# Seven block products in place of eight for the first branch's projection, one half of it moved ahead of the second half's input projection, and the last heads' rows of the second branch in the buffers for rows of x

## The chip, the cores and the metric

The kernel is one program on one core of a Trainium2 chip. The metric is the device time of one execution in microseconds (us), the median over runs. The trace of one profiled execution goes with it; its span runs from the first to the last thing that the profiler recorded.

## What is computed

One layer over 2048 latent tokens of width 1024, with a prefix of 256 context tokens. A combined input projection feeds a gated convolution (branch A) and a bidirectional mLSTM with 8 heads (branch B). Each branch is projected, the two are merged by sigmoid gates, and an output projection, a gated residual and a norm close the layer.

```
hx = rmsnorm(x, g_norm) * (1 + scale) + shift
px = hx @ w_in + b_in
h_x = mlstm_bidir(px[..., :STATE_COLS], ctx_states)      # 8 heads, two directions
...
y_a = b_a * conv * silu(z_a)
y_b = sigmoid(o) * hn * silu(z_b)
merged = sigmoid(g_a) * (y_a @ w_pa) + sigmoid(g_b) * (y_b @ w_pb)
out = x + gate * (merged @ w_out + b_out);  return rmsnorm(out, g_final)
```

All inputs are float32. A dense product is made in three matmul passes on operands split into a rounded high part and a low rest (high by high, high weight by low data, low weight by high data). The split of each operand costs one copy on ScalarE (ACT) and one subtraction on VectorE (DVE): `split`, L178 and L179.

## The kernel before, in words

**Halves and blocks.** The tokens are worked in two halves of 1024 (half 0, half 1), data being held with channels on the partitions. Most dense products are made by `pair` (the matmul is L427): two output tiles of 128 channels for both 512-token column blocks, in seven block products of 12 matmuls instead of eight (Strassen and Winograd's scheme). Its moving operand is an `Operands` object: seven blocks in 28 buffers x0 to x27, loaded by 14 DMAs of 512 KB and 14 splits. The three sums of blocks that this needs are made beforehand by `combine` (L295), which reads a scratch tensor, subtracts on DVE and writes the sums beside it; the sums of weights are made on GpSimd (POOL, L360) in `Stream`. The other form is `slab` (L474): one output tile, for the two column blocks one after the other, 48 matmuls straight from `Branch` (whole rows of y for k = 0 to 7, hi and lo).

**Stages in time.** (1) Input projection of half 0, 44 pairs. Beside it the second half's operands are prepared (`prep_b`, scratch xod), w_out is scaled by the gate (`late_rows`, scratch wod), and the states of the context and of one direction are scanned (`ctx_scan`, `state_scan`, with the state update matmul L658). (2) Input projection of half 1, 44 pairs, beside it `state_scan` and `scan` of half 1 and, for the first EARLY = 3 heads, `scan` of half 0. (3) Four branch products made of slabs: w_pa on half 1 (`PaEnd`), w_pb on half 1 (`PbEnd`), w_pa on half 0, w_pb on half 0, each 8 slabs of 48 matmuls. Beside the first three runs the late `scan` of the remaining five heads of half 0. (4) The output projection in 8 pairs with the residual and the last norm (`output`, `begin`, `close`).

**The order of the work.** On TensorE (PE) the order is the program's order. `run(dense, rate, urate)` writes one dense matmul after the other and puts in between, `rate` steps per matmul, steps of the queue `later` (scans, preparation) and `urate` steps of `urgent` (loads and splits that are needed soon). `flush` empties a queue. On the other engines a scheduler at build time sets the order, save for instructions wrapped in `pin`, which keep the program's. All loads and stores of note go through one DMA queue, that of SyncE (SP), in order.

**Names used below.** `scan` with late=True makes one chunk of 128 tokens of one head in about nine steps: a product of k and q (L834), the weighted values into pn (L891, L892), the normalisation on DVE and ACT (L897 to L905, hb is the result), and after four chunks four transposes (L849), a product with the gate (L851) and a store to ybd (L852). `Branch.fetch` (L1482) loads rows of ybd and splits them. gb and gf (L1554, L1555) are the two rows that the end of the kernel adds and multiplies with; xt are the rows of x that `begin` (L1576) loads for the output, and wod the blocks of w_out. In `output`, L1604 and L1605 add the products to xt, L1607 squares and sums, and `close` (L1596, stores L1597) applies the norm.

## Time and profile before

| what | value |
|---|---|
| median of 3 runs | 2660.72 us (2659.01 to 2660.84) |
| the profiled execution, its time and its span | 2660.47 us, span 2658.7 us |
| PE, DVE, ACT, POOL busy | 2594.5, 1722.6, 1099.0, 1123.8 us |
| matmuls recorded | 12807 |
| mean granted TensorE clock | 0.994 |
| mean DMA rate | 170 GB/s |

The span is 1.8 us shorter than the execution's own time, and that time lies 0.25 us below the median. PE is the engine to read: it is without work for 64 us of the span, at the start, in short waits in stages 1 and 2, at the start of the output stage and behind the last matmul. A row of the timeline has its start, its length, engine, line and tiles; in square brackets stands the engine's idle time before it and what ended that. A matmul's own length overlaps the next one's; what a stage costs is the distance between starts.

### The profile page before, as it was taken

Reading aid. Unit: us, or ns where it says so; the run is one execution under the profiler, and the core shown is the slowest. Engines: PE = TensorE matmul, PEld = TensorE weight load, DVE = VectorE, ACT = ScalarE, POOL = GpSimd, SP = SyncE. Lnnn points to the kernel's source line nnn. Section 1 sums busy time; section 2 is a strip of 40 time slices with the busy share of each in tenths; the row PEclk is TensorE's granted clock in tenths of the full one; section 3 lists DMA queues with packets and bytes.
Section 4 is the critical chain, followed back from the end, with each engine's and each line's share of the span. In section 5 each row is a group of like instructions: output and inputs, shape, how many; then the busy total and the mean of one; then the engine's idle time right before and its main releaser. Section 6 shows DMA issues by size and latency. Waiting matters only on the chain.

```text
span 2658.7 us, 38177 instructions
## 1 busy us (share of the span) xinstructions
PE 2594.5 (98%) x12807; PEld 2166.7 (81%) x12807; DVE 1722.6 (65%) x3119; ACT 1099.0 (41%) x2269; POOL 1123.8 (42%) x1322
## 2 busy tenths in 40 slices
PE   8999999999999999999999999999999999999998
PEld 7788887888878787877887888888888888888777
DVE  6643237687776777478578577667666656554597
ACT  5433344333333335344443444344444544442233
POOL 1221223233345553235555555565555124422674
PEclk9999999999999999999999999999999999999999
DMA  8333344655734457435644653653566978768542
GB/s 231 101 101 106 106 139 131 211 167 179 232 118 123 139 145 236 118 100 159 195 142 130 201 160 120 195 174 128 154 195 201 301 219 273 253 194 288 195 159 96
DMA packets 373217, 452.99 MB, mean 170 GB/s; under 512 B 24428, under 2 KB 273948, under 8 KB 373020
## 3 DMA queue, kind: packets, MB, share of 16 engines
q1 hardware_dynamic: 372784, 450.46, 54.4%
q8 instruction: 102, 1.67, 0.3%
q14 instruction: 95, 0.78, 0.1%
q10 hardware_dynamic: 236, 0.08, 0.0%
HBM read 319.42 MB, written 131.03 MB: 169 GB/s over the span
## 4 chain that ended last, share of the span: by engine, by line
PE 48%; DVE 3%; DMA 2%; issue 1%; POOL 1%; ACT 0%; SPq 0%; DVEq 0%; POOLq 0%; ACTq 0%
PE pd L427 29%; PE pd L474 11%; PE pn L891 2%; PE pn L892 2%; PE pa L834 1%; PE pu L658 1%; DMA mgd<-t2k 1%; DVE wl L179 1%; PE pa L849 1%; PE pn L658 0%; PE pa L669 0%; DVE xt L1596 0%; DVE xt L1605 0%; DMA x<-wod 0%; DVE cv L999 0%
## 5 line engine op out<-in xcount | busy, mean ns | idle before, releaser
L427 PE MATMUL pd<-x,wh 128*128 128x512 f32 x5320 | 1695.9, 397 | 15.9 <-DVE xt L1605 8.5
L427 PEld LDWEIGHTS pd<-x,wh 128*128 128x128 f32 x5320 | 985.1, 189 | 209.9 <-issue 19.4
L427 PE MATMUL pd<-x,wl 128*128 128x512 f32 x2660 | 1057.3, 397 | 0.0
L427 PEld LDWEIGHTS pd<-x,wl 128*128 128x128 f32 x2660 | 501.8, 189 | 99.3 <-issue 0.2
L178 ACT CAST wh<-sw 128x512 fp32r<-128x512 f32 x382 | 237.0, 620 | 492.9 <-PE pd L427 409.0
L179 DVE TENSOR_TENSOR wl<-sw,wh 128x512 fp32r<-128x512 f32 x382 | 303.2, 795 | 182.0 <-ACT wh L178 177.1
L178 ACT CAST wh<-wr 128x512 fp32r<-128x512 f32 x350 | 216.6, 619 | 375.3 <-PE pd L427 269.9
L360 POOL TENSOR_TENSOR sw<-wr,sw 128x512 f32<-128x512 f32 x95 | 136.1, 1433 | 432.6 <-DVE wl L179 345.2
L179 DVE TENSOR_TENSOR wl<-wr,wh 128x512 fp32r<-128x512 f32 x350 | 289.7, 828 | 42.5 <-ACT wh L178 39.1
L474 PE MATMUL pd<-x,wh 128*128 128x512 f32 x896 | 281.7, 396 | 0.0
L360 POOL TENSOR_TENSOR sw<-wr 128x512 f32<-128x512 f32 x95 | 130.9, 1378 | 236.9 <-DVE wl L179 236.0
L653 POOL TENSOR_SCALAR vw<-tk,wk 128x129 f32<-128x129 f32 x205 | 161.9, 794 | 120.2 <-PE pn L658 109.7
L474 PEld LDWEIGHTS pd<-x,wh 128*128 128x128 f32 x896 | 166.3, 188 | 32.1
L474 PE MATMUL pd<-x,wl 128*128 128x512 f32 x448 | 173.4, 397 | 0.0
L186 POOL TENSOR_SCALAR ssq<-ssq 128x1 f32<-128x1 f32 x128 | 37.2, 291 | 293.7 <-ACT hf L906 289.8
L926 DVE TENSOR_TENSOR t2k<-pd,u 128x512 f32<-128x512 f32 x168 | 115.5, 688 | 59.8 <-PE pd L427 59.1
L360 POOL TENSOR_TENSOR sw<-sw,wr 128x512 f32<-128x512 f32 x94 | 132.4, 1408 | 47.9 <-DVE wl L179 37.4
L904 ACT ACTIVATE hf<-pn,rd 128x128 f32<-128x128 f32 x128 | 47.0, 367 | 246.9 <-DVE rd L900 222.4
L360 POOL TENSOR_TENSOR sw<-wr,wr 128x512 f32<-128x512 f32 x94 | 132.2, 1406 | 20.2 <-DVE wl L179 10.8
L820 POOL TENSOR_SCALAR_AFFINE_SELECT mw<-mw 128x256 f32<-128x256 f32 x128 | 61.7, 503 | 119.5 <-DMA mw<-mwd 89.1
L891 PE MATMUL pn<-tk,pt 128*128 128x129 f32 x512 | 98.8, 275 | 5.0 <-DVE hb L905 5.0
L891 PEld LDWEIGHTS pn<-tk,pt 128*128 128x128 f32 x512 | 86.8, 190 | 16.2 <-issue 5.8
(259 smaller groups left out, 3317.5 us busy)
## 6 DMA issues: line engine op xcount, KB each, us to landing
wr<-in_w_in_dram SPq DMA_DIRECT2D x176, 512.0 KB, 4.1
tk<-tokd SPq DMA_DIRECT2D x64, 386.0 KB, 3.6
mw<-mwd SPq DMA_DIRECT2D x44, 512.0 KB, 5.3
qkd<-t2k SPq DMA_DIRECT2D x64, 256.0 KB, 2.9
qk<-qkd SPq DMA_DIRECT2D x64, 256.0 KB, 3.8
tk<-tokd SPq DMA_DIRECT2D x48, 257.0 KB, 2.9
tokd<-t2k SPq DMA_DIRECT2D x32, 258.0 KB, 2.9
x<-in_w_ada_dram SPq DMA_DIRECT2D x16, 512.0 KB, 6.4
```

What stands on the lines that cost most here:

```text
L178: a = nc.scalar.copy(hi, raw)
L179: b = (eng or nc.vector).tensor_tensor(lo, raw, hi.bitcast(F32), op=OP.subtract)
L186: nc.gpsimd.tensor_scalar(dst, ss, 1.0 / n, EPS, op0=OP.mult, op1=OP.add)
L360: nc.gpsimd.tensor_tensor(s, a, b, op=op)
L427: nc.tensor.matmul(ps[b], op[wi][:, kk, :], xs.at(o, xi, kk), start=(fresh and kk + pi == 0), stop=(o == last[b] and kk == 3 and pi == 2), ...
L474: nc.tensor.matmul(pss[j], ops[k // 4][wi][:, k % 4, :], y(xi, k, j), start=(k + pi == 0), stop=(k == NK - 1 and pi == 2))
L653: pin(nc.gpsimd.tensor_scalar(vw, tk[:, VT], wk, None, op0=OP.mult))
L820: pin(nc.gpsimd.affine_select(mws[m][:, :, 0, d, :], mws[m][:, :, 0, d, :], pattern=[[0, 2], [s, P]], base=0, channel_multiplier=-s, compa ...
L891: nc.tensor.matmul(pn[:, d, :], pt[:, d, :], tk[:, VT], start=True, stop=False)
L892: nc.tensor.matmul(pn[:, d, :], qw[:, d, :], cur if d == carried else tk[:, ST], start=False, stop=True)
L904: nc.scalar.activation(hf, pn[:, 0, 0:P], AF.Copy, scale=rd[:, 0:1])
L926: nc.vector.tensor_tensor(t, ps, add, op=OP.add)
```

## The change

- **w_pa in pairs.** `PaEnd` and the slabs of w_pa go. `Gated` makes w_pa by `pair`, four pairs of seven block products for each half, from `Operands` loaded from yad. For this yad is laid out in blocks (`fin_ba` writes it so), and `combine` runs on it for each half, for half 0 with tiles of the pool of stage 1, for half 1 with the five small buffers cv. Each tile of the gate sad is loaded three tiles ahead into cv, and the result goes to mad, now one tensor for each half.
- **Half 0's w_pa moved** into stage 1, behind the input projection of half 0 and ahead of that of half 1. The rate of `later` in stage 1 falls from 0.235 to 0.212. Half 1's w_pa comes behind stage 2, at rate 0.22, and the loads for the next product are spread over its last pair (`arriving`).
- **One more head early.** EARLY is 4, the rate in stage 2 rises from 0.34 to 0.358, and the late scan has four heads. It runs beside w_pa of half 1 (rate 0.22) and w_pb of half 1 (rate 0.55 in place of 0.305).
- **The last branch's rows.** For w_pb on half 0, `Branch` keeps k = 0 to 3 in the x buffers, 4 and 5 in small ones, and 6 and 7 in four of the six xt buffers, whose pool opens when the late scan's pool is closed. Their loads come behind those of gb and gf.
- **The output.** Block 6 of w_out is loaded and split during w_pb of half 0, so four splits are left for the first output pair, not six. Only the first pair's rows of x are loaded ahead; the others follow in the output stage. L1605 is pinned, and in the last pair one `close` is placed after it.

Counted on PE, with like matmuls in a row written together, the program has 11296 rows before and 11200 now.

First place: SP's queue where the last head of the late scan is handed over to w_pb of half 0. The store to ybd is head 7's last; cv, or xk, is where its rows are loaded to. Before:

```order
L852 DMA ybd_135<-g_5885_23848 128x512
L252 DMA x_6023_24497<-wod 128x1024
L1503 DMA mad<-t2k_24315 128x512
L1482 DMA cv_24348<-ybd_135 128x512
L1482 DMA cv_24350<-ybd_135 128x512
L1554 DMA gb<-rowd 128x1024
L1555 DMA gf<-in_g_final_dram 128x1024
```

Now:

```order
L865 DMA ybd_135<-g_6087_24293 128x512
L1558 DMA t2k_24699<-mad_150 128x512
L252 DMA x_6207_24825<-wod 128x1024
L1611 DMA gb<-rowd 128x1024
L1612 DMA gf<-in_g_final_dram 128x1024
L1541 DMA xk_24667<-ybd_135 128x1024
L1541 DMA xk_24670<-ybd_135 128x1024
```

The loads of gb and gf stood behind those of head 7's rows and now stand ahead of them, and head 6's rows have moved down to the same place.

Second place: DVE in the first output pair, from the split of the second block on (x are the blocks of w_out, u the sums inside a pair, wl the low parts of weights). Before:

```order
L179 TENSOR_TENSOR x_6122_25050<-x_6122_25050,x_6120_25048 128x1024
L179 TENSOR_TENSOR x_6125_25053<-x_6125_25053,x_6123_25051 128x1024
L1605 TENSOR_TENSOR xt_24809<-xt_24809,pd_25071 128x512
L179 TENSOR_TENSOR wl_25136<-sw_25133,wh_25135 128x512
L179 TENSOR_TENSOR x_6126_25054<-x_6126_25054,x_6124_25052 128x1024
L179 TENSOR_TENSOR x_6129_25057<-x_6129_25057,x_6127_25055 128x1024
L441 TENSOR_TENSOR u_25156<-pd_25139,u_25107 128x512
L179 TENSOR_TENSOR wl_25159<-wr_25033,wh_25158 128x512
L179 TENSOR_TENSOR x_6130_25058<-x_6130_25058,x_6128_25056 128x1024
L1604 TENSOR_TENSOR xt_24812<-xt_24812,u_25156 128x512
L179 TENSOR_TENSOR wl_25189<-sw_25186,wh_25188 128x512
L1605 TENSOR_TENSOR xt_24812<-xt_24812,pd_25162 128x512
```

Now:

```order
L179 TENSOR_TENSOR x_6298_25351<-x_6298_25351,x_6296_25349 128x1024
L179 TENSOR_TENSOR x_6301_25354<-x_6301_25354,x_6299_25352 128x1024
L1666 TENSOR_TENSOR xt_25216<-xt_25216,pd_25366 128x512
L179 TENSOR_TENSOR wl_25431<-sw_25428,wh_25430 128x512
L179 TENSOR_TENSOR x_6302_25355<-x_6302_25355,x_6300_25353 128x1024
L454 TENSOR_TENSOR u_25455<-pd_25434,u_25402 128x512
L179 TENSOR_TENSOR wl_25458<-wr_25334,wh_25457 128x512
L1665 TENSOR_TENSOR xt_25219<-xt_25219,u_25455 128x512 x2
L1666 TENSOR_TENSOR xt_25219<-xt_25219,pd_25461 128x512
```

Two of the splits ahead of the second addition to xt are gone from here, and one addition of a sum (the x2) has moved up before it.

The diff, cut to its core:

```diff
     def combine(src, tile=None):
...
-            if kk < 4:
+            if kk < 4 and tile is None:
+                bs[kk] = [vslot() for _ in range(4)]
+                for n, t in enumerate(bs[kk]):
+                    ld.dma_start(t, src[n, :, kk, :])
+            elif kk < 4:
                 bs[kk] = [tile([P, 2, NB]) for _ in range(2)]
...
-    yad = scratch("yad", [NK, P, T])
+    yad = scratch("yad", [8, P, 4, NB])
...
-    mad = dp.tile([NK, P, T], F32, name="mad")
+    mad = scratch("mad", [NK, P, T])
...
-                ld.dma_start(yad[half][n, :, S2[j]], v)
+                ld.dma_start(yad[half][2 * (n // 4) + j, :, n % 4, :], v)
...
+    class Gated:
+        def __init__(self, half):
+            self.half = half
+            self.tiles = [(2 * p + i, j) for p in range(4) for i, j in ((0, 0), (1, 1), (1, 0), (0, 1))]
+            self.s = deque()
+        def load(self):
+            if self.tiles:
+                n, j = self.tiles.pop(0)
+                s = vslot()
+                ld.dma_start(s, sad[self.half][n, :, S2[j]])
+                self.s.append(s)
+        def begin(self):
+            self.st = Stream((w_pa, 2 * p * P, True) for p in range(4))
+            self.st.begin()
+            self.y = Operands()
+            self.y.load(yad[self.half], range(7))
+            for _ in range(3):
+                self.load()
+        def pairs(self):
+            for p in range(4):
+                def fin(i, j, ps, add):
+                    s = self.s.popleft()
+                    nc.vector.scalar_tensor_tensor(s, s, 1.0, added(ps, add), op0=OP.add, op1=OP.mult)
+                    ld.dma_start(mad[self.half][2 * p + i, :, S2[j]], s)
+                    self.load()
+                yield pair(self.st, self.y, fin)
...
     for item, fin, w in todo[kv_end:]:
-        run(pair(st, xA, fin), 0.235, 0.5)
+        run(pair(st, xA, fin), 0.212, 0.5)
+        if w == "B3":
+            urgent.append(combine(yad[0], big))
+    flush(urgent)
+    pa = Gated(0)
+    pa.begin()
+    for dense in pa.pairs():
+        run(dense, 0.212, 0.5)
     flush(urgent)
...
-    EARLY = 3
+    EARLY = 4
...
-        run(pair(st, xB, fin), 0.8 if w in ("q0", "o0", "z0") else 0.34, 0.5)
+        run(pair(st, xB, fin), 0.8 if w in ("q0", "o0", "z0") else 0.358, 0.5)
...
+        if w == "B3":
+            urgent.append(combine(yad[1]))
...
-            if self.region == 0 or k < 6:
-                base = 2 * k if self.region == 0 else 16 + 2 * k
-                hi, lo = [xslot(base + p, [P, T], FR) for p in range(2)]
+            whole = (NK, 6, 4)[self.region]
+            if k < whole or self.region == 2 and k > 5:
+                if k < whole:
+                    base = 2 * k if self.region == 0 else 16 + 2 * k
+                    hi, lo = [xslot(base + p, [P, T], FR) for p in range(2)]
+                else:
+                    hi, lo = [so.tile([P, T], FR, tag="xt", name=nm("xk"), bufs=6) for _ in range(2)]
...
-    class PaEnd:
...
-    RATE, URATE = 0.305, 0.3
...
-    run(branch(w_pa, ya, PaEnd, 1), RATE, URATE)
...
-    run(branch(w_pb, yb, PbEnd, 1), RATE, URATE)
...
-    run(branch(w_pa, ya, PaEnd, 0), RATE, 0.5)
+    pa = Gated(1)
+    pa.begin()
+    ya = Branch(0, lambda k: ybd[1][k], ())
+    def arriving():
...
+    for p, dense in enumerate(pa.pairs()):
+        if p == 3:
+            urgent.append(arriving())
+        run(dense, 0.22, 1.0)
+    flush(urgent)
+    yb = Branch(2, lambda k: ybd[0][k], ())
+    urgent.extend(yb.fetch(k, 24) for k in ready)
+    def heads_done(h):
+        if h < 6:
+            urgent.append(yb.fetch(h))
+    run(branch(w_pb, ya, PbEnd, 1), 0.55, 0.5)
     flush(later)
...
-    urgent.extend(load_wo(o) for o in range(4))
-    urgent.extend(begin(m, 6) for m in range(3))
-    run(branch(w_pb, yb, PbEnd, 0), 0, 0.35)
+    last_heads = [yb.fetch(6, 6), yb.fetch(7, 1)]
+    for f in last_heads:
+        next(f)
+    urgent.extend(last_heads)
+    urgent.extend(load_wo(o) for o in (0, 1, 2, 3, 6))
+    urgent.append(begin(0, 6))
+    run(branch(w_pb, yb, PbEnd, 0), 0, 0.36)
...
-                nc.vector.tensor_tensor(xt[:, s], xt[:, s], ps, op=OP.add)
+                pin(nc.vector.tensor_tensor(xt[:, s], xt[:, s], ps, op=OP.add))
+                if m + 1 == len(tiles):
+                    close()
...
-                if m + 1 == len(tiles):
+                if m + 1 == len(tiles) and (i, j) == (0, 1):
                     close()
...
-                if m == 0 and n in (20, 26, 32, 40, 46, 52):
+                if m == 0 and n in (18, 24, 32, 40):
...
-                if n == 34 and m > 0:
-                    for _ in begin(m + 2):
-                        pass
+                if (m, n) in ((0, 44), (1, 8)) or m > 0 and n == 36:
+                    coming.append(begin(len(xts), 16))
+                step(coming)
```

More of the change, by code (lines that the diff above doesn't have):

```diff
@@ L291, in combine @@
         for kk in range(4):
-            load(kk + 1)
-            (b11, b12), (b21, b22) = [(t[:, 0, :], t[:, 1, :]) for t in bs[kk]]
+            if tile is None:
+                yield from gap(8)
+                b11, b12, b21, b22 = bs[kk]
+            else:
+                load(kk + 1)
+                (b11, b12), (b21, b22) = [(t[:, 0, :], t[:, 1, :]) for t in bs[kk]]
             for d, a, b in ((b11, b12, b11), (b12, b22, b12), (b22, b22, b11), (b21, b21, b22)):
@@ L298, in combine @@
             for n, t in enumerate(bs.pop(kk)):
-                ld.dma_start(src[4 + 2 * n:6 + 2 * n, :, kk, :].rearrange("o p i -> p o i"), t)
+                if tile is None:
+                    ld.dma_start(src[4 + n, :, kk, :], t)
+                else:
+                    ld.dma_start(src[4 + 2 * n:6 + 2 * n, :, kk, :].rearrange("o p i -> p o i"), t)
             yield from gap(4)
+            if tile is None:
+                load(kk + 1)
     class Stream:
@@ L1477, in fetch @@
                 for j in range(2):
-                    hi, lo = [slots[4 * (k - 6) + 2 * j + p](FR) for p in range(2)]
+                    hi, lo = [slots[4 * (k - whole) + 2 * j + p](FR) for p in range(2)]
                     parts.append((hi, lo, self.raw(k)[:, S2[j]]))
@@ L1488, in __call__ @@
             return self.t[p, k, j]
-    class PaEnd:
-        def __init__(self, half, n):
-            self.half, self.n, self.s = half, n, {}
-        def begin(self, j):
-            s = self.s[j] = t2k()
-            ld.dma_start(s, sad[self.half][self.n, :, S2[j]])
-        def end(self, j, ps):
-            s = self.s.pop(j)
-            pin(nc.vector.scalar_tensor_tensor(s, s, 1.0, ps, op0=OP.add, op1=OP.mult))
-            ld.dma_start(mad[self.n, :, S2[j]], s)
     class PbEnd:
@@ L1621, in output @@
         parts = []
-        wo.claim(range(4, 7))
-        for o in range(4, 7):
+        wo.claim((4, 5))
+        for o in (4, 5):
             for q in range(2):
```

24 lines of the change are left out of this document (14 added, 10 removed).

## The prediction

> **What bounds the kernel now.** I read the page's head first, then the chain of waits, then the list of waits.
>
> ```profile
> span 2658.7 us, 38177 instructions
> PE 2594.5 (98%) x12807; PEld 2166.7 (81%) x12807; DVE 1722.6 (65%) x3119; ACT 1099.0 (41%) x2269; POOL 1123.8 (42%) x1322
> ```
>
> PE is at work for 98% of the span, so a change can pay in two ways only: fewer matmuls, or less of the 64.2 us in which PE has none. The other engines have a third of their time free or more. The chain has long stretches of nothing but matmuls, such as this one (start, length, instructions):
>
> ```profile
> 2396.25 40.71 PE pd L474 x180
> ```
>
> From this comes the price of one dense matmul. The last of the 180 lasts 0.40 us and overlaps nothing, so (40.71 − 0.40) / 179 = 0.2252 us from start to start. The list of waits then tells for whom PE waits (sum in us, times, longest):
>
> ```profile
> PE pd L427 <- DVE xt L1605: 8.5, 6, 5.0
> PE pn L658 <- DVE tk L662: 7.4, 6, 3.0
> PE pd L427 <- DVE t2k L926: 5.9, 4, 2.6
> PE pn L891 <- DVE hb L905: 5.0, 2, 2.9
> ```
>
> The largest single wait, 5.0 us for L1605, lies in the output stage, in code that the diff touches. The others are DVE waits of 2 to 3 us beside the scans. None of the four names a DMA.
>
> **The change part by part.** All terms are against the profiled execution, 2660.47 us, which lies 0.25 us below the median of the runs shown. A difference of 0.2%, 5.3 us, is about what a measurement of this kernel can tell from none.
>
> *Matmuls.* The order counts 11296 rows on PE before and 11200 now: 96 fewer. That is what the algebra gives, for each half 8 slabs of 48 (384) against 4 pairs of 84 (336). PE has no slack beside it, so 96 × 0.2252 = **−21.6 us**, the one term with little doubt in it. Should one of those stretches be spoilt by waits, that is a term below.
>
> *The first output pair.* Here are PE's rows and DVE's (start, length, and in brackets the idle time before).
>
> ```profile
> 2498.17 0.50 PE L427 MATMUL pd<-x,wh 128*128 128x512 f32 x1 [1.01 <-DVE x L179]
> 2501.64 0.50 PE L427 MATMUL pd<-x,wh 128*128 128x512 f32 x1 [0.45 <-DVE x L179]
> 2502.67 0.39 PE L427 MATMUL pd<-x,wl 128*128 128x512 f32 x1
> 2508.10 1.19 PE L427 MATMUL pd<-x,wh 128*128 128x512 f32 x2 [5.04 <-DVE xt L1605]
> 2511.45 0.40 PE L427 MATMUL pd<-x,wl 128*128 128x512 f32 x1
> ```
>
> ```profile
> 2500.37 3.45 DVE L179 TENSOR_TENSOR x<-x,x 128x1024 fp32r<-128x1024 f32 x2
> 2504.94 1.21 DVE L179 TENSOR_TENSOR x<-x,x 128x1024 fp32r<-128x1024 f32 x1
> 2507.28 0.67 DVE L1605 TENSOR_TENSOR xt<-xt,pd 128x512 f32<-128x512 f32 x1
> ```
>
> PE stops because its next product needs the bank that L1605 at 2507.28 reads, and L1605 stands on DVE behind splits of w_out. By the order two of those go: the pair row of 3.45 becomes one split of 1.21 (−2.2), the row at 2504.94 goes (−1.2). One weight split leaves and one addition of a sum comes in front, 0.6 us each. That is 3.4 us less in front of L1605; I count 3.3, and a gap of 1.7 us is left. Behind the long gap PE was slow as well:
>
> ```profile
> 2508.00:2512.00 4.00, 3.90 (x11) 3.12 (x12) 2.36 (x4) 1.44 (x4) 1.19 (x3) 0.60 0.00 0
> 457.00:460.00 3.00, 3.00 (x9) 2.35 (x8) 2.49 (x4) 2.12 (x4) 0.00 (x0) 0.54 0.03 8
> 456.10 0.96 PE L427 MATMUL pd<-x,wh 128*128 128x512 f32 x2 [2.65 <-DVE t2k L926]
> 1854.10 0.46 PE L891 MATMUL pn<-tk,pt 128*128 128x129 f32 x2 [2.91 <-DVE hb L905]
> ```
>
> In the first two rows the third number from the end is the granted TensorE clock: 0.60 behind the gap of 5.04 us, 0.54 behind one of 2.65. Eight starts from 2508.10 to 2511.45 took 3.35 us in place of 8 × 0.2252 = 1.80, so a slow restart costs 1.55 us. It doesn't follow every gap: after 2.91 us at 1854.10 the first matmul took 0.46 for two, not 0.96. A gap of 1.7 us is under all that were slow, so I let the restart go too: 3.3 + 1.55 = **−4.85 us**. Bounds: 0 if a load of w_out or the sums take DVE's place in front, −6.6 (5.04 + 1.55) if the whole wait goes. The waits of 1.01 and 0.45 are for two of the four splits that are left, and stay.
>
> *The end.* Behind the last matmul DVE does this:
>
> ```profile
> 2650.39 1.41 DVE L1596 SCALAR_TENSOR_TENSOR xt<-xt,sx,gf 128x512 f32<-128x512 f32 x2 [1.84 <-POOL sx L1614]
> 2651.72 0.68 DVE L1605 TENSOR_TENSOR xt<-xt,pd 128x512 f32<-128x512 f32 x1
> ```
>
> The last addition starts 1.33 us after a norm of another tile that it doesn't need. Pinned ahead of it, it can start when the last product is done, a few tenths after 2650.39: **−1.0 us**, bounds −1.33 and 0.
>
> *The hand-over of head 7.* What costs most among the moved steps:
>
> ```profile
> 2395.65 0.60 PE L849 MATMUL pa<-ident,hb 128*128 128x128 f32 x4
> 2397.00 0.32 SPq L852 DMA_DIRECT2D ybd<-g  x1
> 2401.24 0.80 SPq L1482 DMA_DIRECT2D cv<-ybd  x2
> 2403.52 0.46 SPq L252 DMA_DIRECT2D x<-wod  x1
> 2405.31 1.28 DVE L179 TENSOR_TENSOR cv<-cv,cv 128x512 fp32r<-128x512 f32 x2
> 2407.01 1.07 PE L474 MATMUL pd<-cv,wh 128*128 128x512 f32 x4
> 2412.65 1.05 ACT L178 CAST x<-x 128x1024 fp32r<-128x1024 f32 x1 [3.91 <-DMA x<-wod]
> DMA to landing us min/median/max: 3.4/6.1/8.5
> ```
>
> Head 7's transposes are at 2395.65, its store at 2397.00, and the load of its rows could be issued at 2401.24, 5.6 us after the transposes. The splits ended at 2405.31 + 1.28 = 2406.6, just ahead of 2407.01. Already before there was next to no slack. Now the late scan ends nearer to the product: between the transposes and the first matmul on the low part of head 7's rows the order has 44 dense matmuls, where before it has 50. So the rows are due 0.35 + 44 × 0.2252 = 10.3 us after the transposes. And ahead of them SP now issues gb and gf, then the rows of head 6, each 512 KB, as are head 7's: 2.1 MB where there was 0.5 MB. From 2401.24 to 2412.65 the queue moved cv, gb, gf, a tile of sbd and a block of w_out, 2.36 MB in 11.4 us, so 2.1 MB take 10.1 us. Landing is then at 5.6 + 10.1 = 15.7 us, cast and subtraction of a whole row (1.05 + 1.21) end at 18.0, and PE waits 18.0 − 10.3 = 7.7 us, plus 1.55 for the restart: 9.3. The other end: all four land in the median of such loads (last row), 6.1 us, then the stall is 5.6 + 6.1 + 2.3 − 10.3 = 3.7, and 5.2 with the restart. I take **+7.5 us**, nearer to the row of this very place; bounds 0 (the gates' tiles in front of it delay PE less if rows come early) and +11.
>
> The Trainium skill (DMA: Bandwidth & Descriptors, Queues, rings and completion order) says that on each DMA engine descriptors are consumed in ring order, which speaks against this order of loads, and the trace agrees: the block of w_out issued last of its group landed 9.1 us later. Its Specifications section gives about 358 GB/s as the HBM limit of a core, where this stretch moved 207; by that figure, an estimate, the 2.1 MB take 5.9 us, the stall is 3.5 us, the term +5.0 and the time 2.5 us less.
>
> *Swaps of operands.* Pairs need all seven blocks of a new operand in x. Before, stages of pairs met once ahead of the output; now they meet three times, with w_pa of each half between. At the meeting before:
>
> ```profile
> 1030.48 2.22 DVE L179 TENSOR_TENSOR x<-x,x 128x1024 fp32r<-128x1024 f32 x1
> 1033.10 0.67 PE L658 MATMUL pn<-vw,tk 128*128 128x129 f32 x2 [2.96 <-DVE tk L662]
> ```
>
> A split of 2.22 us on DVE stood before the small L662 for which PE waited 2.96 us. Two more meetings could cost 2 × 2.96 = +5.9, or nothing, since splits of one block (1.21 us) usually fit beside 12 matmuls (2.70 us). I take half of one wait: **+1.5 us**.
>
> *The late scan in front of half 0's last product.* Its rows in the three parts of the stage before (columns: PE, PEld, DVE, ACT, POOL busy, clock, DMA share, GB/s), and the DMAs of the whole of it:
>
> ```profile
> 2076.70:2184.00 107.30, 107.30 (x555) 91.19 (x555) 60.25 (x142) 51.19 (x141) 24.69 (x53) 1.00 0.79 247
> 2184.00:2290.00 106.00, 106.00 (x555) 90.21 (x555) 60.60 (x139) 46.83 (x130) 49.90 (x69) 1.00 0.82 265
> 2290.00:2397.00 107.00, 107.00 (x553) 90.84 (x553) 54.87 (x132) 44.25 (x123) 27.14 (x55) 1.00 0.72 221
> DMA packets 60756, 78.31 MB, mean 244 GB/s; under 512 B 3905, under 2 KB 35649, under 8 KB 60730
> tk<-tokd SPq DMA_DIRECT2D x18, 386.0 KB, 3.9
> qk<-qkd SPq DMA_DIRECT2D x18, 256.0 KB, 4.6
> mw<-mwd SPq DMA_DIRECT2D x18, 256.0 KB, 5.9
> ```
>
> Five heads of eight chunks, 40, took 320.3 us: 8.0 us each. The dense part is 3 × 384 × 0.2252 = 259.4 us, so a chunk's own matmuls cost (320.3 − 259.4) / 40 = 1.52 us. At 0.305 steps a matmul that was 351 steps, 8.8 a chunk. In w_pb of half 1 the rate is now 0.55: 211 steps, 24 chunks, in 384 × 0.2252 + 24 × 1.52 = 123 us, or 5.1 us each. Other work per dense matmul stays. The scan's loads, 18 × 898 KB = 16.6 MB, are 21% of the 78.3 MB; with the stores and gates that go with them I reckon a quarter. Chunks come 8.0 / 5.1 = 1.57 times as fast, so the mean DMA share of 0.78 rises by 0.25 × 0.57, to 0.89. It fits, but with little room, and DVE (0.55 busy) has less too. I take **+3.0 us**, as much as one wait like that at 1854.10; bounds 0 and +12 (0.5 us a chunk).
>
> *Sums of blocks and changed rates.* Before, 32 subtractions made such sums; now 64.
>
> ```profile
> L295 DVE TENSOR_TENSOR xb<-xb,xb 128x512 f32<-128x512 f32 x16 | 14.3, 892 | 0.2
> ```
>
> 32 × 0.85 is 27 us of DVE, beside stages that leave it a third. PE waits where one stands ahead of a scan's step. The rates shift scan steps between stages, so a wait of 2.96 may go or two may come: bounds −3 and +5, I take **+1.0 us**.
>
> Sum: −21.6 − 4.85 − 1.0 + 7.5 + 1.5 + 3.0 + 1.0 = −14.45. 2660.47 − 14.45 = 2646.0, and with the 0.25 us to the median 2646.3 us.
>
> **The rivals.**
> - *Everything added is hidden.* Head 7's rows wait behind nothing, the scan is not disturbed: −21.6 − 4.85 − 1.0 = −27.45, 2633.3 us. For it: DMA landing in 6.1 us, all engines but PE a third idle. Against: no slack at 2407.01 even before. Chance 0.15.
> - *DVE turn-taking eats the gain.* Both meetings cost 2.96 us and sums and scan steps meet: swaps +5.9, rates +5.0, hand-over 9.3, the rest as forecast: −21.6 − 4.85 − 1.0 + 9.3 + 5.9 + 3.0 + 5.0 = −4.25, 2656.5 us, within 0.2%. For it: PE's small waits are all on DVE. Chance 0.13.
> - *The late scan cannot go faster, and it is slower than before.* A chunk is a chain of loads, DVE and ACT steps; if it needs the 8.0 us that it had, w_pb of half 1 is 24 × 2.9 = 70 us longer, and the time is 2646.3 − 3.0 + 70 = 2713 us. It decides from (3.0 + 14.45 + 5.3) / 24 = 0.95 us a chunk more, a chunk of 6.0 us. Against: DMA at 0.89, DVE's free third, and no trace of PE waiting for a scan's DMA. Chance 0.05.
> - That the change doesn't do what it says is closed by the 96 rows.
>
> **How the numbers follow.** The forecast has 0.67. Faster by over 0.2% is below 2655.4 us: the forecast's share (0.64 of 0.67), the first rival and 0.05 of the second: 0.84. Within 0.2%: 0.02 of the forecast, 0.07 of the second, 0.01 of the third: 0.10. Slower: 0.06. The range takes in the first rival's time and the second's: 2633 to 2657 us; outside it lie most of the third, and the ends of the first and second, together some 0.17.
>
> **What would show it.** PE's rows: 12711 or near it. A stretch of dense matmuls starts every 0.225 us. In the first output pair the wait for L1605 is about 1.7 us, and the clock behind it stays at 1. The last addition starts ahead of the norm. Between the last transposes and head 7's first matmuls PE waits 3.5 to 8 us for a split of xk, with the clock at about 0.6 behind it. Chunks in w_pb of half 1 come every 5 us. Wrong would be: PE waiting in w_pb of half 1 for pn or a load by tens of us; no wait at the hand-over; waits of 3 us at each new operand.

## The result, and the profile after

The changed kernel takes 2698.26 us (median of 4 runs, 2695.76 to 2703.19), the kernel before 2660.47: a ratio of 1.0145, 95% interval 1.0128 to 1.0163. It is 38 us slower where 14 us faster was forecast. The profiled execution took 2699.76 us, its span is 2698.0. One of the four executions of e9 below took 11823 us; its ratio leaves that one out.

The head of the page, and PE's largest waits (sum in us, times, longest):

```profile
span 2698.0 us, 38358 instructions
PE 2596.6 (96%) x12711; PEld 2157.6 (80%) x12711; DVE 1815.5 (67%) x3225; ACT 1119.2 (41%) x2288; POOL 1191.1 (44%) x1361
```

```profile
PE pn L904 <- DVE hb L918: 15.5, 11, 2.5
PE pn L671 <- DVE tk L675: 13.7, 11, 3.9
PE pd L487 <- ACT xk L178: 9.3, 1, 9.3
PE pd L440 <- DVE xt L1666: 7.7, 5, 4.2
PE pd L440 <- DVE t2k L939: 5.7, 2, 4.4
```

PE has 96 matmuls fewer, as the order said, and yet its busy time is 2.1 us longer: matmuls behind a long wait run at a lower clock (0.59 granted in the last row of this document, 0.54 and 0.60 in the prediction's) and count as busy. So idle time alone doesn't tell what was lost. Here are both kernels by stage, cut near the first dense matmul of each (to 2 us; columns as in the prediction: length, busy time of PE, PEld, DVE, ACT, POOL, granted clock, DMA share, GB/s). Before: the input projections of half 0 and 1, w_pa and w_pb of half 1, w_pa and w_pb of half 0, the output:

```profile
53.70:1042.00 988.30, 968.23 (x4624) 800.52 (x4623) 626.82 (x971) 390.05 (x668) 338.74 (x325) 0.99 0.47 145
1042.00:2075.60 1033.60, 1019.31 (x5146) 853.67 (x5146) 706.38 (x1472) 453.77 (x1004) 537.00 (x682) 1.00 0.53 163
2075.60:2181.90 106.30, 106.30 (x549) 90.34 (x548) 60.03 (x141) 50.66 (x137) 23.63 (x50) 1.00 0.80 249
2181.90:2290.30 108.40, 108.40 (x567) 92.21 (x566) 62.22 (x141) 48.45 (x134) 50.96 (x71) 1.00 0.82 262
2290.30:2397.00 106.70, 106.70 (x552) 90.62 (x551) 54.57 (x132) 44.25 (x123) 27.14 (x55) 1.00 0.72 221
2397.00:2483.80 86.80, 86.80 (x384) 71.87 (x383) 35.86 (x42) 18.84 (x26) 38.32 (x23) 1.00 0.81 268
2483.80:2658.70 174.90, 156.82 (x676) 126.97 (x675) 147.67 (x164) 64.20 (x131) 97.36 (x89) 0.97 0.40 141
```

After: the input projection of half 0, w_pa of half 0, the input projection of half 1, w_pa and w_pb of half 1, w_pb of half 0, the output:

```profile
52.20:1023.00 970.80, 959.79 (x4583) 794.66 (x4583) 625.05 (x954) 388.15 (x667) 329.81 (x305) 1.00 0.50 152
1023.00:1117.60 94.60, 86.18 (x384) 70.39 (x383) 69.26 (x110) 34.09 (x48) 40.05 (x36) 0.96 0.79 251
1117.60:2187.20 1069.60, 1041.93 (x5246) 868.74 (x5245) 744.13 (x1551) 467.21 (x1050) 563.31 (x724) 0.99 0.58 172
2187.20:2276.50 89.30, 88.10 (x430) 73.23 (x429) 69.71 (x124) 45.12 (x101) 33.81 (x39) 1.00 0.76 242
2276.50:2423.70 147.20, 131.49 (x702) 110.20 (x700) 88.13 (x226) 73.91 (x224) 72.44 (x117) 0.97 0.81 249
2423.70:2524.10 100.40, 91.09 (x386) 73.49 (x384) 38.12 (x43) 19.63 (x26) 32.57 (x21) 0.95 0.74 241
2524.10:2698.00 173.90, 157.32 (x674) 127.54 (x672) 152.07 (x162) 62.31 (x129) 108.56 (x92) 0.97 0.40 138
```

For the losses each stage is cut at its first dense matmul exactly, by count of the dense matmuls. From its length I take what its matmuls ask for: 0.2252 us for a dense one, and 0.122 us for any other, which is what is left for them in the three stages of before in which PE never waits. The rest is the stage's loss, in waits and slow restarts together:

| stage | loss before, us | loss after, us |
|---|---|---|
| start | 14.8 | 13.2 |
| input projection, half 0 | 43.3 | 30.0 |
| w_pa of half 0, between them | | 13.3 |
| input projection, half 1 | 24.8 | 48.9 |
| w_pa of half 1 | −0.2 | 2.4 |
| w_pb of half 1 | −0.4 | 22.2 |
| w_pa of half 0, as slabs | −0.1 | |
| w_pb of half 0 | 0.6 | 14.2 |
| output | 22.8 | 22.3 |

The losses grow from 105.6 to 166.5 us, 60.9 us; less the 21.6 us of the 96 matmuls that is 39.3, and the spans differ by 39.3. So the saving is there, and is spent almost three times over, in three places: around w_pa of half 0 (the input projections with it: +24.1), in w_pb of half 1 (+22.6), and at the hand-over to w_pb of half 0 (+13.6). In the runs below the losses of stages that were left alone differ by up to 5 us from run to run.

**The late scan.** One of seven like waits in w_pb of half 1:

```profile
2282.55 2.35 DVE L179 TENSOR_TENSOR x<-x,x 128x1024 fp32r<-128x1024 f32 x2
2284.82 0.15 DVE L910 SCALAR_TENSOR_TENSOR den<-pn,em 128x2 f32<-128x2 f32 x1
2286.02 0.35 DVE L918 SCALAR_TENSOR_TENSOR hb<-pn,rd,hf 128x128 f32<-128x128 f32 x1 [0.52 <-ACT hf L917]
2286.42 0.78 PE L904 MATMUL pn<-tk,pt 128*128 128x129 f32 x2 [2.50 <-DVE hb L918]
```

Two subtractions for an operand stand on DVE in front of the small steps from pn to hb. PE has come round to the next chunk before these are done. The seven waits add up to 12.5 us.

**The hand-over.** Head 7's transposes, its store, the loads of gb and of the two heads' rows, and PE's wait:

```profile
2423.33 0.60 PE L862 MATMUL pa<-ident,hb 128*128 128x128 f32 x4
2426.09 0.62 SPq L865 DMA_DIRECT2D ybd<-g  x1
2431.96 0.32 SPq L1611 DMA_DIRECT2D gb<-rowd  x1
2432.80 0.90 SPq L1541 DMA_DIRECT2D xk<-ybd  x2
2440.30 2.14 ACT L178 CAST xk<-xk 128x1024 fp32r<-128x1024 f32 x2 [5.46 <-DMA xk<-ybd]
2441.40 1.22 PE L487 MATMUL pd<-xk,wh 128*128 128x512 f32 x2 [9.28 <-ACT xk L178]
```

What SP itself waited for (2425.9 to 2434 us; sum in us, times, longest):

```profile
SPq L1611 <- DMA ybd<-g: 3.6, 1, 3.6
```

The first of the four loads, that of gb, is held until head 7's store has landed, 5.8 us after its issue. So store and loads follow one another.

**New operands.** Where half 1's operand takes the place of that of w_pa, and behind it:

```profile
1112.01 0.94 PE L440 MATMUL pd<-x,wh 128*128 128x512 f32 x2 [4.35 <-DVE t2k L939]
1121.95 0.50 PE L440 MATMUL pd<-x,wl 128*128 128x512 f32 x1 [2.18 <-DVE wl L179]
1140.79 1.12 PE L682 MATMUL pa<-ident,t2k 128*128 128x128 f32 x4 [3.75 <-DVE t2k L946]
1105.00:1115.00 10.00, 5.65 (x20) 4.29 (x19) 9.35 (x12) 5.68 (x8) 2.19 (x1) 0.86 0.81 244
```

DVE is busy 9.35 of these 10 us while PE waits for it.

### The profile page after: what moved, and what is told of

Read it like the earlier page. It is cut to its first block, busy times and chain, and to the rows that moved or that the text cites. A ratio compares the mean times of both kernels' runs of the same rounds, so it can differ in the third digit from the quotient of the medians.

```text
span 2698.0 us, 38358 instructions
## 1 busy us (share of the span) xinstructions
PE 2596.6 (96%) x12711; PEld 2157.6 (80%) x12711; DVE 1815.5 (67%) x3225; ACT 1119.2 (41%) x2288; POOL 1191.1 (44%) x1361
## 5 line engine op out<-in xcount | busy, mean ns | idle before, releaser
L440 PEld LDWEIGHTS pd<-x,wh 128*128 128x128 f32 x5768 | 1078.1, 189 | 230.4 <-issue 12.7
L440 PE MATMUL pd<-x,wl 128*128 128x512 f32 x2884 | 1145.3, 397 | 2.5 <-DVE wl L179 2.5
L440 PEld LDWEIGHTS pd<-x,wl 128*128 128x128 f32 x2884 | 546.2, 189 | 108.4 <-DVE wl L179 3.4
L178 ACT CAST wh<-sw 128x512 fp32r<-128x512 f32 x414 | 256.3, 619 | 532.8 <-PE pd L440 450.1
L179 DVE TENSOR_TENSOR wl<-sw,wh 128x512 fp32r<-128x512 f32 x414 | 326.3, 789 | 180.9 <-ACT wh L178 178.2
L939 DVE TENSOR_TENSOR t2k<-pd,u 128x512 f32<-128x512 f32 x192 | 131.9, 687 | 70.8 <-PE pd L440 68.7
L373 POOL TENSOR_TENSOR sw<-sw,wr 128x512 f32<-128x512 f32 x102 | 146.2, 1433 | 49.5 <-DVE wl L179 37.2
L373 POOL TENSOR_TENSOR sw<-wr,wr 128x512 f32<-128x512 f32 x102 | 146.6, 1437 | 23.9 <-DVE x L179 10.5
L179 DVE TENSOR_TENSOR x<-x,x 128x1024 fp32r<-128x1024 f32 x68 | 94.2, 1396 | 31.9 <-ACT x L178 31.7
L946 DVE SCALAR_TENSOR_TENSOR t2k<-pd,cols,u 128x512 f32<-128x512 f32 x73 | 54.7, 750 | 78.9 <-PE pd L440 77.0
```

The costliest lines, as they stand in the source:

```text
L178: a = nc.scalar.copy(hi, raw)
L179: b = (eng or nc.vector).tensor_tensor(lo, raw, hi.bitcast(F32), op=OP.subtract)
L373: nc.gpsimd.tensor_tensor(s, a, b, op=op)
L440: nc.tensor.matmul(ps[b], op[wi][:, kk, :], xs.at(o, xi, kk), start=(fresh and kk + pi == 0), stop=(o == last[b] and kk == 3 and pi == 2), ...
L939: nc.vector.tensor_tensor(t, ps, add, op=OP.add)
L946: nc.vector.scalar_tensor_tensor(dst, ps, bcol(col), add, op0=OP.add, op1=OP.add)
```

## The experiments

All but e9 change the changed kernel in one thing, e5 and e12 with the rates that go with it. Losses of stages are worked out as above. e7 and e13 leave out the product of w_pa that the reference has. Their times, the kernel before being run beside each (2659.8 to 2661.4 us):

| run | us | ratio to the kernel before (95%) |
|---|---|---|
| e1 even rate | 2690.11 | 1.0113 (1.0097 to 1.0130) |
| e2 rows first | 2692.86 | 1.0125 (1.0109 to 1.0141) |
| e3 rows of x later | 2700.33 | 1.0156 (1.0137 to 1.0174) |
| e5 w_pa of half 0 behind | 2689.24 | 1.0114 (1.0097 to 1.0131) |
| e6 row splits on POOL | 2695.70 | 1.0127 (1.0110 to 1.0143) |
| e7 no new operand | 2679.99 | 1.0065 (1.0050 to 1.0080) |
| e8 scan done early | 2685.40 | 1.0085 (1.0069 to 1.0100) |
| e9 behind, three early | 2696.56 | 1.0127 (1.0102 to 1.0152) |
| e10 half the splits on POOL | 2707.48 | 1.0179 (1.0159 to 1.0199) |
| e11 rates turned round | 2694.76 | 1.0134 (1.0112 to 1.0156) |
| e12 six heads early | 2696.35 | 1.0128 (1.0102 to 1.0154) |
| e13 splits, no loads | 2701.00 | 1.0154 (1.0137 to 1.0171) |

### The rate of the late scan

e1:

```diff
-        run(dense, 0.22, 1.0)
+        run(dense, 0.397, 1.0)
-    run(branch(w_pb, ya, PbEnd, 1), 0.55, 0.5)
+    run(branch(w_pb, ya, PbEnd, 1), 0.397, 0.5)
```

> The changed kernel with one thing undone in part: the late scan's steps are spread evenly, 0.397 a matmul beside w_pa of half 1 and beside w_pb of half 1, in place of 0.22 and 0.55. In the changed kernel w_pb of half 1 takes 146.8 us where dense matmuls and the scan's own ask for 124: 22 us are lost there. Theory (steps too close): PE comes back for a scan buffer before DVE and ACT have worked through the chain from pn to hb; at 0.397 the loss in w_pb of half 1 falls from 22 to 6 us or less, w_pa of half 1 gets 60 steps more and loses no more than 5 us more, and the whole is 12 to 18 us shorter, 2680 to 2686 us. Rival (operand splits): the loss comes from the splits of ybd's rows on DVE beside that product, which stay; then the loss stays above 15 us and the whole falls by less than 6 us.

Half of it came: w_pb of half 1 loses 11.9 us, w_pa of half 1 8.4, the whole is 8.2 us shorter. Neither theory's numbers hold. The rate counts, but the two products together lose 20.3 us in place of 24.6: the loss moves rather than goes. About as much was won at the hand-over, where w_pb of half 0 loses 9.8 us in place of 14.2.

e11, 0.50 and 0.305 at the same two places:

> The changed kernel with the two rates of the late scan turned round: 0.50 beside w_pa of half 1 (pairs) and 0.305, the rate of the kernel before, beside w_pb of half 1. Theory (the rate makes the loss, wherever it is): w_pb of half 1 loses 5 us or less in place of 22, w_pa of half 1 loses 15 to 20 us in place of 2, and the whole changes by less than 5 us. Rival (what lies beside the scan in w_pb of half 1, the splits of ybd's and w_out's rows, makes the loss): w_pb of half 1 still loses 12 us or more, and the whole is 10 us or more longer, over 2706 us.

w_pb of half 1 loses 8.8 us at the rate at which the kernel before lost nothing, w_pa of half 1 loses 15.2, and the whole is 3.5 us shorter. So the loss follows the rate, but some of it stays: 5.41 us of the 8.8 is one wait for hb. The result lies between the two theories.

e6:

```diff
-                split(hi, lo, lo.bitcast(F32), pinned=wait > 0)
+                split(hi, lo, lo.bitcast(F32), nc.gpsimd if self.region == 2 else None, pinned=wait > 0)
```

> The changed kernel with the subtractions for the rows of ybd (the operand of the last branch product, 1.2 to 2.4 us each) made on POOL in place of DVE. In the changed kernel each of the seven waits for hb in w_pb of half 1 has such a subtraction, of rows of ybd or of w_out, on DVE or its cast on ACT between pn and hb. Theory (operand splits in front of the chain): w_pb of half 1 loses 10 us or less in place of 22, since only the splits of w_out stay on DVE, and the whole is 8 to 14 us shorter, 2684 to 2690 us. Rival (steps too close, whatever DVE does beside them): the loss stays above 17 us and the whole changes by less than 5 us; it could also be longer, if POOL's subtractions slow DVE.

w_pb of half 1 loses 19.6 us; the rival's numbers hold. PE's waits in it (2275.08 to 2419.7 us):

```profile
PE pn L904 <- DVE hb L918: 6.8, 3, 3.7
PE pu L671 <- ACT vw L664: 6.0, 6, 1.7
```

In the changed kernel they were 12.5 and 3.1 us: those for hb were nearly halved, and those for vw doubled. In front of the two longest that are left, 2.49 and 3.67 us, DVE still has splits that the edit didn't move: those of w_pb's own rows, and one of a block of w_out. So the run doesn't show that splits are harmless; it shows that moving one kind of them changes little.

e12:

```diff
-    EARLY = 4
+    EARLY = 6
-        run(pair(st, xB, fin), 0.8 if w in ("q0", "o0", "z0") else 0.358, 0.5)
+        run(pair(st, xB, fin), 0.8 if w in ("q0", "o0", "z0") else 0.408, 0.5)
-            if r < EARLY:
-                later.append(scan(sp_, [r], 0))
+            for h in ([0], [1], [2, 4], [3, 5])[r]:
+                later.append(scan(sp_, [h], 0))
-        run(dense, 0.22, 1.0)
+        run(dense, 0.235, 1.0)
-    run(branch(w_pb, ya, PbEnd, 1), 0.55, 0.5)
+    run(branch(w_pb, ya, PbEnd, 1), 0.235, 0.5)
```

> The changed kernel with six heads of half 0's scan in half 1's input projection in place of four (rate 0.408 in place of 0.358), so that the late scan has two heads, at 0.235 beside w_pa and w_pb of half 1, and ends 101 rows ahead of the first matmul on head 6's rows. Theory (steps too close, and a hand-over too late): the two products lose 6 us or less together in place of 25, w_pb of half 0 2 us in place of 14, half 1's input projection loses no more than 8 us more, and the whole is 20 to 32 us shorter, 2666 to 2678 us. Rival (a scan step costs PE waits at any rate): the losses move into half 1's input projection, which loses 15 us more or over, and the whole is above 2682 us.

w_pb of half 1 loses 5.3 us, w_pa of half 1 3.3 and w_pb of half 0 1.8, near what the theory said. But half 1's input projection loses 74.0 us in place of 48.9. Its end is unlike that of any other run: at 0.408 the scan isn't done when the last product is, and PE makes the rest of it with no dense matmul in between.

```profile
2223.37 0.77 PE L904 MATMUL pn<-tk,pt 128*128 128x129 f32 x2 [4.00 <-DVE hb L918]
2230.49 0.80 PE L904 MATMUL pn<-tk,pt 128*128 128x129 f32 x2 [5.05 <-DVE hb L918]
```

From 2217.62 to the next dense matmul at 2237.00 that is 19.4 us for 28 small matmuls, 16.0 of it loss. Without it the projection would lose 58.0 us, 9 more than with four heads early, and the whole would take 2680 us (an estimate, 2696.35 − 16.0), between the theory's 2678 and the rival's 2682. The time is the rival's, but steps left over at this rate made much of it, so the run doesn't decide between the two.

### The hand-over

e2 issues gb and gf behind the rows of heads 6 and 7:

```diff
-    ld.dma_start(gb_t, rowd)
-    ld.dma_start(gf_t, bass.AP(tensor=g_final.tensor, offset=g_final.offset, ap=[[0, P], [1, D]]))
...
     for f in last_heads:
         next(f)
+    ld.dma_start(gb_t, rowd)
+    ld.dma_start(gf_t, bass.AP(tensor=g_final.tensor, offset=g_final.offset, ap=[[0, P], [1, D]]))
     urgent.extend(last_heads)
```

> The changed kernel with the loads of gb and gf moved behind those of the rows of heads 6 and 7 on SP's queue. Theory (queue): the 1 MB ahead delays the rows; in the changed kernel they are issued 9.5 us after head 7's transposes and land at 17.0 us. Without it head 6's rows don't wait for head 7's store, land some 5 us earlier, head 7's some 2 us earlier; PE's wait of 9.28 us falls to about 5 to 6 us and the whole by 3 to 5 us. Rival (store): the landing is set by the store of head 7's rows alone; the wait stays above 8 us and the whole changes by less than 1.5 us.

PE's wait fell from 9.28 to 6.36 us, the stage's loss from 14.2 to 10.3, the whole by 5.4 us. The queue theory holds for its part; the larger part stays. What it had wrong is that head 6's rows wouldn't wait for head 7's store: SP waited 4.0 us for that store ahead of the rows here as it had ahead of gb, and it took 6.2 us to land.

e8 is the changed kernel with 0.45 in both places of e1:

> The changed kernel with the late scan at 0.45 steps a matmul beside w_pa and w_pb of half 1, so that head 7's transposes come 120 rows ahead of the first matmul on head 6's rows in place of 37. Theory (hand-over): head 7's rows are stored long before they are loaded, PE's wait of 6 to 9 us for xk goes to 1 us or less, w_pb of half 0 loses 2 us or less in place of 11 to 13; the scan's own losses in the two products before are as with an even 0.397, about 21 us together, so the whole is 16 to 20 us shorter than the changed kernel, 2678 to 2683 us. Rival (the loads wait for the pool or the queue, not for head 7): the wait stays above 5 us and the whole is like that of the even rate, 2690 us.

Head 7's transposes and PE's matmuls on the rows:

```profile
2403.44 0.60 PE L862 MATMUL pa<-ident,hb 128*128 128x128 f32 x4
2423.24 1.99 ACT L178 CAST xk<-xk 128x1024 fp32r<-128x1024 f32 x2
2430.90 1.09 PE L487 MATMUL pd<-xk,wh 128*128 128x512 f32 x4
```

The rows are cast 7.7 us before PE comes to them, there is no wait left, and the stage loses 1.8 us. The whole is 12.9 us shorter, somewhat less than expected, since w_pa and w_pb of half 1 lose 24.8 us together at 0.45. That the hand-over cost some 12 us is shown.

### New operands of pairs

e5 takes `pa = Gated(0)` and its loop out of stage 1 and runs both halves' pairs behind stage 2:

```diff
-        run(pair(st, xA, fin), 0.212, 0.5)
+        run(pair(st, xA, fin), 0.235, 0.5)
...
+    for half in range(2):
+        pa = Gated(half)
+        pa.begin()
+        for p, dense in enumerate(pa.pairs()):
+            if half == 1 and p == 3:
+                urgent.append(arriving())
+            run(dense, 0.271, 1.0)
...
-    run(branch(w_pb, ya, PbEnd, 1), 0.55, 0.5)
+    run(branch(w_pb, ya, PbEnd, 1), 0.271, 0.5)
```

> The changed kernel with half 0's w_pa moved back behind the second half's input projection, ahead of half 1's, both still in pairs; the rate in the input projection of half 0 is 0.235 as in the kernel before, and the late scan is spread over all three products at 0.271. Theory (each new operand for pairs costs PE waits, and steps too close cost more): the stretch from the start of half 0's input projection to the end of half 1's loses 60 us as in the kernel before in place of 76, w_pb of half 1 loses under 5 us in place of 22, the two products in pairs about 14 together as now 20: 2698 - 16 - 18 - 6 = 2658, with 2650 to 2672 as bounds. Rival (the extra early head and the 64 more sums and splits on DVE cost the time wherever they stand): the input projections lose 70 us or more, and the whole stays above 2675 us.

2689 us: the rival. The two input projections lose 80.8 us without a product between them (before 68.1), w_pa of half 0 3.4, and w_pa of half 1 14.2, most of it one wait of 11.50 us for a weight's low part where the two products in pairs meet. Together that is 98.4 us, where the changed kernel loses 94.6 in the same products: the place of w_pa of half 0 hardly matters, a meeting costs wherever it is.

e7 multiplies w_pa with the operand that is there:

```diff
-            self.y = Operands()
-            self.y.load(yad[self.half], range(7))
+            self.y = xB if self.half else xA
```

> The changed kernel with both runs of w_pa in pairs multiplied with the operand that already lies in the x buffers (that of the input projection of the same stretch), so that the 14 loads and 14 splits of each new operand are left out, and what is computed there isn't the reference's product; the second half's rows are still loaded. Theory (each new operand for pairs costs PE waits): w_pa of half 0 loses 3 us or less in place of 13 to 17, w_pa of half 1 2 us or less in place of 3 to 7, the last part of the input projection before each loses less too; the start of half 1's input projection keeps its waits. The whole is 12 to 22 us shorter, 2676 to 2686 us. Rival (it is the scan beside w_pa, or DVE's gates and sums): the losses stay, and the whole falls by less than 5 us.

18.3 us shorter, as the theory said. But w_pa of half 0 still loses 8.7 us where 3 or less were expected; 5.31 of it is a wait at its end, where half 1's operand comes in.

e10 moves half of the subtractions for new operands to POOL:

```diff
-    def load_split(hi, lo, raw):
+    def load_split(hi, lo, raw, eng=None):
...
-        split(hi, lo, lo.bitcast(F32))
+        split(hi, lo, lo.bitcast(F32), eng)
...
-                    load_split(self.t[o][0][q], self.t[o][1][q], src[self.PLACE[o], :, 2 * q:2 * q + 2, :])
+                    load_split(self.t[o][0][q], self.t[o][1][q], src[self.PLACE[o], :, 2 * q:2 * q + 2, :], nc.gpsimd if q else None)
```

> The changed kernel with every second subtraction for a new operand of pairs made on POOL in place of DVE (7 of 14 for each operand). Where a new operand comes in, DVE is busy 9 of 10 us in the changed kernel and POOL 1 to 2. Theory (DVE is what is full there): the stretch from the input projection of half 0 to the end of half 1's, which loses 90 to 95 us, loses 10 us or more less, and the whole is 8 to 15 us shorter, 2683 to 2690 us. Rival (the loads come too late, or DVE and POOL slow each other as in the output): the stretch loses within 4 us of what it did, or more, and the whole changes by less than 4 us or is longer.

9.2 us longer; half 1's input projection loses 54.1 us. The rival holds, without telling which of its two reasons.

e13 separates loads from work:

```diff
-            self.y = Operands()
-            self.y.load(yad[self.half], range(7))
+            self.y = xB if self.half else xA
+            for o in range(7):
+                for q in range(2):
+                    hi, lo = (self.y.t[o][p][q] for p in range(2))
+                    split(hi, lo, lo.bitcast(F32))
```

> The changed kernel with the 14 loads of the new operand left out at both runs of w_pa in pairs, while its 14 casts and 14 subtractions are made, in place, on the operand that lies in the x buffers; what is computed there isn't the reference's product. Leaving out loads, casts and subtractions together made the kernel 18 us shorter. Theory (DVE and ACT work at the meeting is what PE waits for): the time comes back, 2692 us or longer, and w_pa of half 0 loses 12 us or more. Rival (the loads land too late): it stays as without any of them, 2684 us or shorter, and w_pa of half 0 loses 10 us or less. Between the two: each has its part.

The time came back in full, 2701.0 us. The same 10 us of both kernels, e7 first, then e13, and e13's wait:

```profile
1010.00:1020.00 10.00, 10.00 (x49) 8.25 (x48) 5.39 (x13) 3.83 (x7) 3.60 (x5) 1.00 0.77 237
```

```profile
1010.00:1020.00 10.00, 10.00 (x48) 8.06 (x47) 10.00 (x16) 9.25 (x12) 6.38 (x5) 1.00 0.39 129
1027.18 0.80 PE L440 MATMUL pd<-x,wl 128*128 128x512 f32 x1 [6.62 <-DVE wl L179]
```

In e13 DVE is busy all 10 us and ACT 9.25, with a DMA share of only 0.39, and PE then waits 6.62 us for a weight's low part that stands behind the splits, at the third matmul of w_pa of half 0. That product loses 16.7 us, over the 12 expected. So the casts and subtractions are enough to make PE wait, with no load of theirs. That the loads have no part in the changed kernel isn't shown. There the casts come no earlier than the loads let them; ACT's waits for the operand of w_pa of half 0 (995 to 1125 us):

```profile
ACT x L178 <- DMA x<-yad: 11.1, 10, 4.5
```

Where half 1's input projection, the stage whose loss grew most, loses its time can be read off by groups of four of its 44 pairs (us). The other seven groups differ little: they lose 15.2 us together before and 16.6 after.

| pairs | before | after | e7 | e13 | e9 |
|---|---|---|---|---|---|
| 1 to 4 | 9.1 | 18.6 | 12.1 | 17.7 | 9.9 |
| 13 to 16 | −0.1 | 3.7 | 3.1 | 2.8 | −0.1 |
| 37 to 40 | 0.3 | 3.9 | 5.3 | 3.9 | 8.6 |
| 41 to 44 | 0.0 | 6.0 | −0.1 | 5.1 | 6.6 |

The first group grows only where w_pa in pairs stands ahead of it, the last only where a new operand for w_pa follows it. In the changed kernel the 16 subtractions for the sums of half 1 (2001.55 to 2046.7) lie in the third row's pairs, and that growth is there without the operand too (e7). The second row's growth is missing in e9, which has three heads early. For these two rows the cause is argued from the place: no run took the sums away alone.

### The output

e3:

```diff
-                if (m, n) in ((0, 44), (1, 8)) or m > 0 and n == 36:
+                if (m, n) in ((0, 66), (1, 8)) or m > 0 and n == 36:
```

> The changed kernel with the loads of the second pair's rows of x, and with them the two additions of gb on POOL, begun 22 matmuls later in the first output pair (at 66 in place of 44). In the changed kernel two additions on DVE (L1665) took 3.43 us while POOL's addition of gb (L1637, 5.41 us for two) ran beside them, and PE waited 4.21 us for L1666. Theory (DVE and POOL slow each other): without POOL's addition the pair takes 1.3 us, the wait falls to about 2 us with a fast restart, the whole by 2 to 4 us. Rival (order of DVE): the pair waits for a product or a split; then the wait stays near 4 us and the whole changes by less than 1 us.

The changed kernel's first output pair, then that of e3:

```profile
2532.75 4.55 DVE L179 TENSOR_TENSOR x<-x,x 128x1024 fp32r<-128x1024 f32 x2
2533.38 6.18 POOL L1637 TENSOR_TENSOR xt<-xt,gb 128x1024 f32<-128x1024 f32 x2 [1.10 <-DMA xt<-in_x_dram]
2537.82 2.30 DVE L179 TENSOR_TENSOR wl<-sw,wh 128x512 fp32r<-128x512 f32 x1
2542.88 3.43 DVE L1665 TENSOR_TENSOR xt<-xt,u 128x512 f32<-128x512 f32 x2
2546.95 1.22 PE L440 MATMUL pd<-x,wh 128*128 128x512 f32 x2 [4.21 <-DVE xt L1666]
```

```profile
2530.21 2.35 DVE L179 TENSOR_TENSOR x<-x,x 128x1024 fp32r<-128x1024 f32 x2
2533.08 0.68 DVE L179 TENSOR_TENSOR wl<-sw,wh 128x512 fp32r<-128x512 f32 x1
2536.52 3.46 DVE L1665 TENSOR_TENSOR xt<-xt,u 128x512 f32<-128x512 f32 x2
2540.63 0.73 PE L440 MATMUL pd<-x,wh 128*128 128x512 f32 x2 [2.26 <-DVE xt L1666]
2565.78 1.19 PE L440 MATMUL pd<-x,wh 128*128 128x512 f32 x2 [5.79 <-DVE xt L1666]
```

Where POOL's addition of gb no longer runs beside them, two splits take 2.35 us in place of 4.55 and a weight's subtraction 0.68 in place of 2.30, and the first pair's wait falls to 2.26 us with a quick restart. But the second pair then waits 5.79 us for its own rows, and the whole is unchanged within the interval. The theory holds for the mechanism, not for the time: a later addition is late for the next pair. POOL's other additions still ran beside the two L1665, which stayed at 3.46.

### A version from all of it

e9 takes e5 and e6 together with EARLY = 3, the rate 0.34 in stage 2, 0.365 beside the three products, and one stream of weights for both halves' w_pa:

> What the runs so far point to, in one kernel: both products w_pa in pairs behind the second half's input projection, with one stream of weights for the two; three heads early with the rates of the kernel before (0.235 and 0.34); the late scan of five heads at 0.365 beside the three products, so that it ends ahead of the hand-over; rows of ybd split on POOL. The theory of three losses (meetings of operands, splits in front of the scan's chain, a hand-over too late): the input projections lose 69 us as in the kernel before, the two products in pairs 10, w_pb of half 1 5, the hand-over 1, the output 22: 2660.5 - 21.6 + 16 = 2655 us, bounds 2648 to 2665. Rival (pairs beside the scan lose by DVE's load itself): the two products in pairs lose 20 us or more, and the whole is 2667 us or longer.

2696.56 us, and 2692.61 without its longest run. The hand-over costs nothing (1.8), w_pb of half 1 loses 4.9, but the two products in pairs lose 16.3 and 17.7 us beside the scan, and half 1's input projection 40.6. The rival holds; 9.50 of the 17.7 us is one wait for hb where the two products meet, with splits of the new operand on DVE between its steps. No version here beats the kernel before; the nearest whole one is e8.

## Why the prediction was wrong, point by point

The saving held, and the terms for the waits failed. In the measured losses the late scan cost 22.6 us where 3.0 were put on it, the new operands with sums and rates 26.8 where 2.5 were, the hand-over 13.6 where 7.5 were, and the output gave back 0.5 where 5.85 were hoped for.

- *96 matmuls, −21.6 us.* Right: 12807 recorded before, 12711 now, and at 0.2252 us each the stages' losses and the spans agree.
- *The first output pair, −4.85, and the end, −1.0.* The output's loss fell by 0.5 us in all. At the end the last norm starts 3.2 us after the last matmul in place of 4.0, near the forecast. The pair failed at "the pair row of 3.45 becomes one split of 1.21": I took DVE's times from a pair in which POOL adds nothing. The change moves the addition of gb for later rows of x from the product before into this pair, which I had seen and not priced, and beside it DVE's subtractions took 4.55 us in place of 2.35 and 2.30 in place of 0.68. The wait is 4.21 us in place of 5.04, and the slow restart stays.
- *The hand-over, +7.5.* The mechanism was right, the size was 13.6 us. The step that was short is that "the load of its rows could be issued at 2401.24, 5.6 us after the transposes": the store was issued 2.8 us after them in place of 1.35, took 5.8 us to land, and gb, which I had let go ahead, waited for that and was issued only 8.6 us after the transposes. From then to the cast of the rows it took 8.3 us (2431.96 to 2440.30), for 2.1 MB about 252 GB/s in place of my 207. The Trainium skill (DMA: Bandwidth & Descriptors, Specifications) gives about 358 GB/s as the HBM limit of a core; these loads stayed below it.
- *Swaps of operands, +1.5, and sums and rates, +1.0.* The stretch of the input projections with both products w_pa lost 94.6 us in place of 67.8, +26.8. Of these e7 shows some 18 to come with the new operands of w_pa (loads, casts and subtractions), and e13 that the casts and subtractions alone cost as much. What failed is "two more meetings could cost 2 × 2.96": I priced a meeting by its one largest wait. It is 14 casts and 14 subtractions on top of DVE's and ACT's own work in some 30 us, with several waits, each with a slow restart, and it falls on dense results and weights too, not on scan steps alone. The second rival had this mechanism, but with that same price. The sums and the fourth early head were mis-sized as well, if the table of pairs is read rightly: 3.6 and 3.8 us of that stage's growth stand where they are. The rate of stage 1 worked the other way. With 0.212 half 0's input projection loses 27 to 31 us in all runs, with 0.235 42 to 43 (before, e5, e9); that made up for the 13.3 us of w_pa of half 0.
- *The late scan, +3.0.* It lost 22.6 us. The third rival had put the turning point at 6.0 us a chunk; 24 chunks in 147.2 us are 6.1. I had argued from shares of DMA and of DVE. They stayed at 0.81 and 0.60, and that says nothing on how long a chain of small steps takes to get through an engine's queue when two splits, 2.35 us together, are ahead of it. That the rate sets the loss is shown by e1 and e11; that the splits in front of the chain do is read from the trace, and e6 moved only part of them. The trace of before had the same thing at another place: L662 behind a split of 2.22 us.

Still open is how the rest of half 1's input projection's growth (24.8 to 48.9 us) divides between the sums, the fourth early head and the operands: the table of pairs gives the places, but no run took the sums or the head away alone.

## What to carry to other kernels

Fewer matmuls don't pay where what feeds them shares an engine with a chain that PE waits for. An operand that serves few products (here four pairs, 10.8 us saved) can cost nearly as much in waits around its splits, here about 9 us, before its sums are counted. A busy share well below one doesn't make room: look for the longest instruction that can stand in front of a short chain, and at how long PE takes to come back to it. An addition on POOL is not free beside DVE, and a product's last-made rows need a lead as long as store, load and split together.

## What the runs showed of the hardware

DVE slows in steps beside POOL's additions of 128x1024: 0.68 us became 2.30, and 2.35 became 4.55, for operations that read two tiles of SBUF. An L1666, which reads one of its two operands from PSUM, took 0.68 us in between (2537.22). The Trainium skill (SBUF — State Buffer, two separate sides) says that such an operation and one on POOL share a pair of ports by an exclusive lock for a whole instruction; the trace agrees, with 1.6 us more for one subtraction beside additions of 2.4 to 3.1 us. e6 and e10, which gave DVE's subtractions to POOL, changed the time by −2.6 and +9.2 us.

PE's slow restart also follows gaps that I had thought too short. After the wait of 2.18 us at 1121.95 the clock was 0.59:

```profile
1122.00:1125.00 3.00, 3.00 (x8) 2.38 (x9) 0.49 (x1) 0.92 (x1) 0.00 (x0) 0.59 0.98 369
```

The wait of 2.26 us in e3 had none (two matmuls in 0.73 us). Waits of about 2 us can thus go either way. A slow restart adds some 1.5 us to its wait, an estimate from the 1.55 us worked out in the prediction.
